# Reciprocal roots in the scan stage of a hybrid encoder block: Ln, Exp and a Newton step in place of GpSimd's power

## The chip, the cores and the metric

The kernel runs on one core of a Trainium2 chip. The core has five instruction queues that run side by side: TensorE (PE in the profile, with its weight loads as PEld), VectorE (DVE), ScalarE (ACT), GpSimd (POOL) and SyncE (SP), which here only issues DMAs. Each queue works in order; a semaphore makes an instruction of one queue wait for one of another. The metric is the device time of one execution in microseconds, as the median of several executions.

## The reference

One layer of a hybrid encoder block on x of 1 x 1024 x 1024 in float32:

```python
h = rmsnorm(x, norm_mix_w)
z, xbc, dt_raw, q, k, v = split(h @ w_in)
y_ssm = ssd_mixer(z, xbc, dt_raw, ...)          # bidirectional scan in chunks of 128
y_na = neighbourhood_attention(q, k, v, ...)    # 16 heads of 64
x = x + concat([y_ssm, y_na]) @ w_out
h = rmsnorm(x, norm_mlp_w)
out = x + square(relu(h @ w_mlp_in)) @ w_mlp_out
```

Two norms inside it matter here. The scan's output is gated and normed by groups of 512 channels, and q and k are normed by heads of 64:

```python
g = y.reshape(bsz, t, SSM_GROUPS, gw) * silu(z).reshape(bsz, t, SSM_GROUPS, gw)
g = g * rsqrt(mean(g * g, axis=-1, keepdims=True) + EPS)     # gw = 512, EPS = 1e-5

q = rmsnorm(q.reshape(bsz, t, NA_HEADS, 64), q_norm_w) * 64 ** -0.5
k = rmsnorm(k.reshape(bsz, t, NA_HEADS, 64), k_norm_w)
```

## The kernel before

The 1024 tokens are eight blocks of 128, one token to a partition. Float32 products are made of three matmuls on operands split into a high and a low part (`mm3`, L177 to L180): ScalarE copies the high part, VectorE or GpSimd subtracts it to get the low one (L148 and L149 for weights, L184 to L190 for what comes out of PSUM).

The work goes in stages. First the norm of x and its transposes; then the projection of the convolved channels and the decays (`decays`, where Exp, Ln and Exp run on ScalarE at L386, L410 and L416); then the projection of z, sixteen blocks whose output goes through Silu (L509). After that comes the stage that the change touches. Two kinds of work run in it together:

- The scan. Eight steps of `backward` and `forward` (L677 to L680), each for two groups. A `backward` step loads the running sums of the decays (`rb`, L605), subtracts on GpSimd (L612), selects on VectorE (L618), takes Exp on ScalarE (L623), multiplies on VectorE (L625) and multiplies by the inputs on TensorE (`pd`, L630). `carried` brings in the state of the chunk before (`py`, then `yo`, L567), `decay_state` makes the next one (`xw` on GpSimd at L653 or L672, `pS` on TensorE, `st` at L549 and L550, its split at L553 and L554). Where both directions have come together, `gated` multiplies by the gate (L574), squares and sums on ScalarE (L576), takes the reciprocal root (`ry`, one number to a token), scales (L578) and stores. It runs sixteen times, in the second half of the scan.
- The projections of q, k and v (`qkv_proj`), 48 blocks of 24 matmuls each into PSUM tiles `pq`, of which three are in rotation. Each of the 32 blocks of q and k goes through `normed_split`: Square on ScalarE (L695), a reduction over each head on VectorE (L697), the reciprocal root (`rq`, eight numbers to a token), the scaling on VectorE that reads `pq` for the last time (L699), four transposes on TensorE (`ptq`, L705) and a split (L187, L188). ScalarE's queue then issues the stores (L717, L723, L732).

Both reciprocal roots come from `inv_rms` (L199 to L203): two GpSimd instructions, a scale-and-add (L201) and a power with exponent -0.5 (L202). The same function serves the norm ahead of the MLP (`r0`, L1080), which the change leaves as it is.

The order of each engine's instructions is not written out in the kernel. A scheduler that comes with the language works it out when the kernel is built, from the order of the program's lines as priority and from its own estimate of each instruction's time (`schedule_with_timeline_sim=True`, L1373); `tc.issue_after(ins)` puts what is traced under it behind `ins` on that engine. So on TensorE the scan's matmuls and the projections' stand interleaved in one fixed order, and a matmul whose operand comes late holds up all behind it. The neighbourhood attention, the output projection and the MLP follow after about 670 us.

ScalarE holds one set of function tables at a time; where the next function isn't in it, the build puts in a table load (`ACT_TABLE_LOAD`).

Of the kernel before, what the change touches and what calls it, by code (L numbers as in the profile page):

```python
# [9 lines left out]
F32 = mybir.dt.float32  # L10
# [3 lines left out]
AF = mybir.ActivationFunctionType  # L14
# [4 lines left out]
P = 128  # L19
# [7 lines left out]
EPS = 1e-5  # L27
NEG = -1.0e30
HD = 64


def shape_constants():
# [23 lines left out]
def hymba_block(  # L56
# [25 lines left out]
    nc = tc.nc  # L82
    mul, add, sub = ALU.mult, ALU.add, ALU.subtract
# [22 lines left out]
    def ps_mm(name="mm"):  # L106
        return phase["ps"].tile([P, 512], F32, tag="mm", name=name, bufs=phase["mm"])

    def ps_tp(name="tp"):
        return ps.tile([P, 512], F32, tag="tp", name=name, bufs=2)  # L110
# [6 lines left out]

    q_dr = dr.tile([8, 4, HD, T], F32, name="q_dr")
    k_dr = dr.tile([2, 2, 4, P, T], F32, name="k_dr")
    v_dr = dr.tile([NT, P, 16, 2, HD], F32, name="v_dr")  # L120
    sz_dr = dr.tile([NT, P, D], F32, name="sz_dr")
# [32 lines left out]
    def load_w_nat(src, r0, nk, c0, lo_eng):  # L154
        tiles = []
        for k2 in range(nk // 2):
            v = src[r0 + 256 * k2 : r0 + 256 * (k2 + 1), c0 : c0 + 512]
            tiles.append(load_w(v.rearrange("(a p) f -> p a f", p=P), lo_eng))

        def get(k):  # L160
            hi, lo = tiles[k // 2]
            s = slice((k % 2) * 512, (k % 2) * 512 + 512)
            return hi[:, s], lo[:, s]

        return get
# [11 lines left out]
    def mm3(pt, ah, al, bh, bl, first, last):  # L177
        nc.tensor.matmul(pt, lhsT=ah, rhs=bh, start=first, stop=False)  # L178
        nc.tensor.matmul(pt, lhsT=ah, rhs=bl, start=False, stop=False)  # L179
        return nc.tensor.matmul(pt, lhsT=al, rhs=bh, start=False, stop=last)  # L180

    def split_from_psum(hi, lo, src, scalar=None):
        if scalar is None:
            nc.scalar.activation(hi, src, AF.Copy)  # L184
            nc.vector.tensor_tensor(lo, src, hi.bitcast(F32), op=sub)
        else:
            nc.scalar.activation(hi, src, AF.Copy, scale=scalar)  # L187
            nc.vector.scalar_tensor_tensor(  # L188
                lo, src, scalar, hi.bitcast(F32), op0=mul, op1=sub
            )  # L190
# [8 lines left out]
    def inv_rms(pool, ss, n, width, tag):  # L199
        r = pool.tile([P, width], F32, tag=tag, name=tag, bufs=2)  # L200
        nc.gpsimd.tensor_scalar(r, ss, 1.0 / n, EPS, op0=mul, op1=add)  # L201
        nc.gpsimd.tensor_tensor(r, r, half[:, 0:width], op=ALU.pow)  # L202
        return r  # L203

    def transpose_split(th, tl, t, hn):
# [13 lines left out]
    with ExitStack() as ph:  # L219
        enter_phase(ph, 1, 3, 1)  # L220
        hp = ph.enter_context(tc.tile_pool(name="hp", bufs=1))
# [15 lines left out]
        rcol = cp.tile([P, NT], F32, name="rcol")  # L237
# [48 lines left out]
        for j in range(2):  # L286
            nc.sync.dma_start(prow[80:81, j * HD : (j + 1) * HD], q_norm_w)
            nc.sync.dma_start(prow[81:82, j * HD : (j + 1) * HD], k_norm_w)
        pp = ps_tp("pp")
# [3 lines left out]
        nc.vector.tensor_scalar(  # L293
            pcol[:, 80:81], pcol[:, 80:81], HD**-0.5, None, op0=mul
        )
# [15 lines left out]
        with ExitStack() as p1:  # L311
            qp = p1.enter_context(tc.tile_pool(name="qp", bufs=2, side="right", reuse_waits="tile"))

            rrow = qp.tile([P, T], F32, name="rrow", bufs=1)
            for h in range(2):
# [5 lines left out]
                    op=mul,  # L321
# [179 lines left out]
            for g in range(2):  # L501
                get = load_w_nat(w_in[0], 0, KD, OFF_Z + 512 * g, nc.vector)
                for t in range(NT):
                    pt = ps_mm("pz")
                    for k in range(KD):
                        s = (slice(None), k, slice(t * P, (t + 1) * P))
                        mm3(pt, hTh[s], hTl[s], *get(k), k == 0, k == KD - 1)
                    zs = qp.tile([P, 512], F32, tag="zs", name="zs")
                    nc.scalar.activation(zs, pt, AF.Silu, scale=rcol[:, t : t + 1])  # L509
                    nc.scalar.dma_start(szb[:, t, :, g * 512 : (g + 1) * 512], zs)  # L510

        def hb(v):
            return v.unsqueeze(2).broadcast_to([P, 8, HD])

        def h8(v):
            return v.rearrange("p (e d) -> p e d", d=HD)

        with ExitStack() as p2:
            qp = p2.enter_context(tc.tile_pool(name="qs", bufs=2, side="right", reuse_waits="tile"))
            zt = qp.tile([P, 192], F32, tag="y1", name="zt")  # L520
            nc.gpsimd.memset(zt, 0.0)
            for r0 in (0, 23):
# [47 lines left out]
            def gated(y1, c, g):  # L570
                gs = slice(g * 512, (g + 1) * 512)
                sz = qp.tile([P, 512], F32, tag="sz", name="sz")
                nc.sync.dma_start(sz, sz_dr[c, :, gs])
                nc.vector.tensor_tensor(y1, y1, sz, op=mul)  # L574
                ss = qp.tile([P, 1], F32, tag="ss", name="ss")
                nc.scalar.activation(sz, y1, AF.Square, accum_out=ss)  # L576
                r = inv_rms(qp, ss, 512, 1, "ry")
                nc.scalar.activation(y1, y1, AF.Copy, scale=r)  # L578
                nc.scalar.dma_start(y_dr[c, :, gs], y1)

            def backward(c, g):
# [61 lines left out]
                if c >= NT // 2:  # L643
                    nc.scalar.dma_start(y1_dr[c, :, g * 512 : (g + 1) * 512], y1)
                else:
                    if c > 0:
                        yf = qp.tile([P, 512], F32, tag="yo", name="yf", bufs=1)
                        nc.sync.dma_start(yf, y1_dr[c, :, g * 512 : (g + 1) * 512])
                        nc.gpsimd.tensor_tensor(y1, y1, yf, op=add)
                    gated(y1, c, g)  # L650
# [42 lines left out]
            def normed_split(pt, rt, w):  # L693
                qn = hp.tile([P, 512], F32, tag="qn", name="qn", bufs=2)
                nc.scalar.activation(qn, pt, AF.Square, scale=rt)  # L695
                ss = hp.tile([P, 8], F32, tag="sq", name="sq", bufs=2)
                nc.vector.tensor_reduce(ss, h8(qn), axis=mybir.AxisListType.X, op=add)  # L697
                r = inv_rms(hp, ss, HD, 8, "rq")
                nc.vector.scalar_tensor_tensor(  # L699
                    h8(qn), h8(pt), rt, hb(r), op0=mul, op1=mul  # L700
                )
                tp = ps_tp("ptq")
                for j in range(4):
                    s = slice(j * P, (j + 1) * P)
                    nc.tensor.transpose(tp[:, s], qn[:, s], ident)  # L705
                hl = hp.tile([P, 2, 512], F32R, tag="hl", name="hl", bufs=2)
                split_from_psum(hl[:, 0], hl[:, 1], tp, w)
                return hl.bitcast(F32).rearrange("f a (p t) -> f a p t", p=4)
# [64 lines left out]
    with ExitStack() as ph:  # L773
# [292 lines left out]
        for t in (0, 4, 1, 5, 2, 6, 3, 7):  # L1066
            xt = x2[:, t, :]
            for h, get in enumerate((get0, get1)):
                pt = ps_mm("po")
                s = slice(t * P, (t + 1) * P)  # L1070
                for k in range(4):
                    yh, yl = last[k]
                    mm3(pt, yh[:, s], yl[:, s], *get(k), k == 0, k == 3)
                d = xt[:, h * 512 : (h + 1) * 512]
                nc.vector.tensor_tensor(d, d, pt, op=add)
            nc.sync.dma_start(x2_dr[t], xt)
            jk = np_.tile([P, D], BF16, tag="jk", name="jk", bufs=1)
            ss = np_.tile([P, 1], F32, tag="ss", name="ss")
            nc.scalar.activation(jk, xt, AF.Square, accum_out=ss)
            r = inv_rms(np_, ss, D, 1, "r0")  # L1080
            nc.vector.scalar_tensor_tensor(xt, xt, r, wb, op0=mul, op1=mul)
            if before is not None:
                factors(before)
            before = t
# [163 lines left out]
    with ExitStack() as ph:  # L1248
# [32 lines left out]
        for fb in range(4):  # L1281
# [18 lines left out]
            for i in ORD:  # L1300
# [14 lines left out]
                for t in range(4):  # L1315
                    pt = (X if i in (1, 6, 7, 4) else Y)[t]
# [60 lines left out]
```

## Time and profile before

| what | us |
|---|---|
| median of three executions | 1728.23 (1726.64 to 1728.27) |
| the profiled execution | 1725.33 |
| its span, from the first instruction to the last | 1723.5 |
| the stage of the change in it | about 270 to 650 |

The span is what the profile's rows are taken from; the 1.8 us between it and the profiled execution's time lie around it. "Busy" is the time in which an engine works on an instruction; "idle before" a group is the time its engine sat unoccupied just ahead of it, and the arrow names what ended most of it. A busy TensorE is not one at its peak, since its matmuls are pipelined and their ends are modelled. Of the chain of work that ended last, which the page follows back from the last instruction, 16% of the span is TensorE's in the MLP.

### The profile page before, as it was taken

To read this page: it belongs to the slowest core of one execution; us is meant where nothing else is said; L and a number is where in the kernel's file an instruction comes from. 1 tells how busy PE (TensorE), PEld (TensorE's weight loads), DVE (VectorE), ACT (ScalarE), POOL (GpSimd) and SP (SyncE) were. 2 spreads that over 40 slices of the span, in tenths; PEclk is the share of its full clock that TensorE was granted. 3 is DMA by queue.
4 is the path that set the end of the run, shared out by engine and by line. 5 is a ranking of instruction groups with operands and counts; after the bars stand their busy time and mean duration, and the time that the engine had idled before them with its cause. 6 is when DMAs were issued, how large, how long until landed. Compare 5 with 4: busy or idle time off the path is not lost. (4 is left out here: it accounts for less than half of the span.)

```text
span 1723.5 us, 20879 instructions
## 1 busy us (share of the span) xinstructions
PE 1636.0 (95%) x7461; PEld 1304.6 (76%) x7461; DVE 1106.3 (64%) x1687; ACT 726.5 (42%) x1189; POOL 705.6 (41%) x496
## 2 busy tenths in 40 slices
PE   6999999989888999999999988999999978999999
PEld 5788888777766777777767767788888866888887
DVE  5767214889787744778787776454343359787863
ACT  5434223434344434555565533454444443333330
POOL 4000004888778741221242242244444426555551
PEclk9999999999998999999999999999999989999999
DMA  8213338876675796754453141254344394644231
GB/s 200 62 37 104 89 98 242 210 195 207 213 206 161 234 311 199 240 150 138 132 183 123 56 159 49 73 190 153 134 159 147 125 349 149 201 141 166 92 110 73
DMA packets 178499, 269.75 MB, mean 157 GB/s; under 512 B 13963, under 2 KB 105051, under 8 KB 178395
## 3 DMA queue, kind: packets, MB, share of 16 engines
q1 hardware_dynamic: 135419, 231.18, 42.6%
q10 hardware_dynamic: 42976, 37.23, 7.1%
q8 instruction: 59, 0.97, 0.2%
q14 instruction: 45, 0.37, 0.1%
HBM read 185.21 MB, written 86.50 MB: 158 GB/s over the span
## 5 line engine op out<-in xcount | busy, mean ns | idle before, releaser
L760 POOL TENSOR_TENSOR wl<-wraw,wh 128x1024 fp32r<-128x1024 f32 x110 | 300.1, 2740 | 350.1 <-ACT wh L759 336.7
L745 PE MATMUL px<-wh,ahl 128*128 128x512 f32 x512 | 163.7, 397 | 9.8 <-ACT ahl L759 9.8
L759 ACT ACTIVATE wh<-wraw 128x1024 fp32r<-128x1024 f32 x110 | 115.7, 1054 | 127.4 <-issue 42.4
L179 PE MATMUL pq<-wl,hTh 128*128 128x512 f32 x384 | 153.1, 400 | 4.6 <-DVE wl L149 4.4
L745 PE MATMUL px<-h,wh 128*128 128x512 f32 x496 | 156.5, 396 | 0.0
L178 PE MATMUL pq<-wh,hTh 128*128 128x512 f32 x384 | 153.1, 401 | 1.9 <-ACT wh L148 1.2
L180 PE MATMUL pq<-wh,hTl 128*128 128x512 f32 x384 | 151.9, 396 | 0.0
L759 ACT ACTIVATE ahl<-ar 128x1024 fp32r<-128x1024 f32 x56 | 58.9, 1053 | 173.0 <-PE px L745 89.6
L760 DVE TENSOR_TENSOR ahl<-ar,ahl 128x1024 fp32r<-128x1024 f32 x56 | 107.3, 1917 | 37.4 <-ACT ahl L759 36.2
L745 PEld LDWEIGHTS px<-wh,ahl 128*128 128x128 f32 x512 | 97.3, 190 | 31.9 <-ACT ahl L759 10.2
L745 PEld LDWEIGHTS px<-h,wh 128*128 128x128 f32 x496 | 93.4, 189 | 22.4
L149 DVE TENSOR_TENSOR wl<-wraw,wh 128x1024 fp32r<-128x1024 f32 x40 | 55.0, 1376 | 83.3 <-ACT wh L148 82.7
L878 POOL TENSOR_TENSOR mb<-braw,nam 128x256 f32<-128x256 f32 (+1 forms) x48 | 41.0, 884 | 159.7 <-DVE nmx L936 123.4
L184 ACT ACTIVATE pth<-ptp 128x384 fp32r<-128x384 f32 (+1 forms) x128 | 58.4, 459 | 107.8 <-PE ptp L959 106.8
L745 PE MATMUL px<-wl,ahl 128*128 128x512 f32 x256 | 100.9, 394 | 0.0
L745 PE MATMUL px<-h,wl 128*128 128x512 f32 x248 | 98.1, 396 | 0.0
L179 PEld LDWEIGHTS pq<-wl,hTh 128*128 128x128 f32 x384 | 73.2, 191 | 22.1 <-DVE wl L149 7.9
L149 POOL TENSOR_TENSOR wl<-wraw,wh 128x1024 fp32r<-128x1024 f32 x18 | 43.8, 2446 | 110.5 <-ACT wh L148 84.3
L745 PE MATMUL pz<-wh,ahl 128*128 128x512 f32 x256 | 82.8, 400 | 6.5 <-DVE acc L1330 5.0
L178 PEld LDWEIGHTS pq<-wh,hTh 128*128 128x128 f32 x384 | 72.9, 190 | 18.2 <-ACT wh L148 2.5
L180 PEld LDWEIGHTS pq<-wh,hTl 128*128 128x128 f32 x384 | 73.2, 191 | 14.7
L612 POOL TENSOR_TENSOR rb<-rb,c 128x512 f32<-128x512 f32 x64 | 75.0, 1192 | 21.5 <-DMA rb<-cum_dr 18.7
(265 smaller groups left out, 4242.6 us busy)
## 6 DMA issues: line engine op xcount, KB each, us to landing
act_dr<-cq SPq DMA_DIRECT2D x56, 512.0 KB, 3.0
ar<-act_dr SPq DMA_DIRECT2D x56, 512.0 KB, 3.8
wraw<-in_w_in_dram SPq DMA_DIRECT2D x44, 512.0 KB, 4.0
rb<-cum_dr SPq DMA_DIRECT2D x32, 512.0 KB, 7.6
wraw<-in_w_mlp_in_dram SPq DMA_DIRECT2D x32, 512.0 KB, 4.7
wraw<-in_w_mlp_out_dram SPq DMA_DIRECT2D x32, 512.0 KB, 5.3
q_dr<-hl ACTq DMA_DIRECT2D x64, 128.0 KB, 3.2
k_dr<-hl ACTq DMA_DIRECT2D x16, 512.0 KB, 3.2
```

The source lines that it names most:

```text
L149: lo_eng.tensor_tensor(lo[:, 0:n], raw[:, 0:n], hi[:, 0:n].bitcast(F32), op=sub)
L178: nc.tensor.matmul(pt, lhsT=ah, rhs=bh, start=first, stop=False)
L179: nc.tensor.matmul(pt, lhsT=ah, rhs=bl, start=False, stop=False)
L180: return nc.tensor.matmul(pt, lhsT=al, rhs=bh, start=False, stop=last)
L184: nc.scalar.activation(hi, src, AF.Copy)
L612: nc.gpsimd.tensor_tensor(rb[:, d], rb[:, d], c1[:, d, c, h0 : h0 + 4].unsqueeze(2).broadcast_to([P, 4, P]), op=sub,)
L745: nc.tensor.matmul(pt, lhsT=a, rhs=b, start=f, stop=l, skip_group_check=True)
L759: nc.scalar.activation(hl[0], src, AF.Copy)
L760: eng.tensor_tensor(hl[1], src, hl[0].bitcast(F32), op=sub)
L878: nc.gpsimd.tensor_tensor(mb[:, s].rearrange("p (s r c) -> p s r c", r=16, c=8), v[:, a:b], nam[:, s].rearrange("p (s r c) -> p s r c", r= ...
```

## The change

A second function for the reciprocal root is added, and the two norms of the scan stage call it. It takes ln of the mean square plus EPS, then exp of -0.5 times that, and improves the result r of the argument s by one Newton step, r (1.5 - 0.5 s r r). `ss` is written over on the way. Ahead of it all, a load of the table set with number 6 (`LN_EXP`), which serves both functions, is put on ScalarE behind the last Silu of the z projection.

```diff
+LN_EXP = 6
...
+    def inv_rms_newton(pool, ss, n, width, tag):
+        r = pool.tile([P, width], F32, tag=tag, name=tag, bufs=2)
+        nc.vector.tensor_scalar(ss, ss, 1.0 / n, EPS, op0=mul, op1=add)
+        nc.scalar.activation(r, ss, AF.Ln)
+        nc.scalar.activation(r, r, AF.Exp, scale=-0.5)
+        nc.vector.scalar_tensor_tensor(ss, ss, -0.5, r, op0=mul, op1=mul)
+        nc.vector.tensor_tensor(ss, ss, r, op=mul)
+        nc.vector.scalar_tensor_tensor(r, ss, 1.5, r, op0=add, op1=mul)
+        return r
...
-                    nc.scalar.activation(zs, pt, AF.Silu, scale=rcol[:, t : t + 1])
+                    last_silu = nc.scalar.activation(zs, pt, AF.Silu, scale=rcol[:, t : t + 1])
...
+            with tc.issue_after(last_silu.ins):
+                nc.scalar.add_instruction(
+                    mybir.InstLoadActFuncSet(
+                        act_func_set_id=LN_EXP,
+                        name=nc.get_next_instruction_name(),
+                        engine=mybir.EngineType.Activation,
+                    )
+                )
...
-                r = inv_rms(qp, ss, 512, 1, "ry")
+                r = inv_rms_newton(qp, ss, 512, 1, "ry")
...
-                r = inv_rms(hp, ss, HD, 8, "rq")
+                r = inv_rms_newton(hp, ss, HD, 8, "rq")
```

## The prediction

> **What bounds the kernel now.** The page comes first: its busy shares, then the span in 40 slices of 43 us, from which these rows matter.
>
> ```profile
> PE 1636.0 (95%) x7461; PEld 1304.6 (76%) x7461; DVE 1106.3 (64%) x1687; ACT 726.5 (42%) x1189; POOL 705.6 (41%) x496
> ...
> PE   6999999989888999999999988999999978999999
> ...
> DVE  5767214889787744778787776454343359787863
> ...
> POOL 4000004888778741221242242244444426555551
> ```
>
> TensorE is busy nearly everywhere. Slices 7 to 14 (about 270 to 650 us) are the scan stage: there PE drops to 8 while VectorE and GpSimd both stand at 7 and 8. So PE sets the pace and this stage makes it wait. The next view is the busy time of each engine in stretches (columns: stretch and length, then busy us and instructions of PE, PEld, DVE, ACT, POOL; granted clock; DMA).
>
> ```profile
> 270.00:430.00 160.00, 147.66 (x730) 119.16 (x730) 129.21 (x193) 61.48 (x104) 127.05 (x112) 1.00 0.79 224
> 430.00:490.00 60.00, 53.18 (x248) 41.39 (x247) 48.65 (x68) 25.25 (x46) 40.53 (x39) 1.00 0.68 207
> 490.00:610.00 120.00, 106.77 (x499) 85.71 (x498) 89.96 (x135) 48.69 (x93) 99.65 (x98) 0.94 0.70 207
> 610.00:650.00 40.00, 39.34 (x181) 31.31 (x180) 17.58 (x21) 14.66 (x22) 13.65 (x15) 1.00 0.94 298
> ```
>
> PE is idle for 12.3 + 6.8 + 13.2 + 0.7 = 33.1 us of these 380. That is all that a change of the norms can give back in the stage. Summed in the same way, DVE is busy 285.4 us and idle 94.6, POOL is busy 280.9, ACT 150.1. Who ends PE's idle time is in the list of waits, cut to 270 to 650 us (us in total, times, longest).
>
> ```profile
> PE pcb L587 <- DVE yo L567: 7.5, 4, 3.1
> PE pd L630 <- DVE rb L625: 7.3, 9, 1.3
> PE pq L179 <- DVE wl L149: 4.4, 5, 1.7
> PE py L178 <- DVE yo L567: 2.5, 2, 2.0
> PE ptq L705 <- DVE qn L699: 1.8, 5, 0.9
> ```
>
> The largest waits all end with a VectorE instruction, and only the last row, 1.8 us, is the norm's own consumer. So the question is what makes VectorE late. There are two kinds of lateness; the timeline has an example of each.
>
> ```profile
> 360.51 1.68 POOL L202 TENSOR_TENSOR rq<-rq,half 128x8 f32<-128x8 f32 x1
> ...
> 362.23 0.75 DVE L699 SCALAR_TENSOR_TENSOR qn<-pq,rcol,rq 128x512 f32<-128x512 f32 x1 [0.93 <-POOL rq L202]
> ...
> 363.03 0.66 PE L705 MATMUL ptq<-ident,qn 128*128 128x128 f32 x4 [0.94 <-DVE qn L699]
> ```
>
> Here a power on GpSimd ends, VectorE had sat 0.93 us for it, and TensorE 0.94. This kind the change removes.
>
> ```profile
> 407.47 0.67 DVE L697 TENSOR_REDUCE sq<-qn 128x8 f32<-128x512 f32 x1
> ...
> 408.06 1.46 DVE L149 TENSOR_TENSOR wl<-wraw,wh 128x1024 fp32r<-128x1024 f32 x1
> ...
> 409.58 0.50 PE L179 MATMUL pq<-wl,hTh 128*128 128x512 f32 x1 [1.73 <-DVE wl L149]
> ```
>
> Here VectorE had no idle time: it worked its queue off, and TensorE lost 1.73 us to a weight's split that came behind a norm's reduction. This kind the change feeds.
>
> **The change, part by part.** Removed from GpSimd, from the groups by line (count, then busy us, mean ns, idle before):
>
> ```profile
> L202 POOL TENSOR_TENSOR rq<-rq,half 128x8 f32<-128x8 f32 x32 | 54.4, 1701 | 1.7
> L201 POOL TENSOR_SCALAR rq<-sq 128x8 f32<-128x8 f32 x32 | 13.2, 413 | 17.5 <-DVE sq L697 15.4
> L202 POOL TENSOR_TENSOR ry<-ry,half 128x1 f32<-128x1 f32 x16 | 10.2, 637 | 0.8
> L201 POOL TENSOR_SCALAR ry<-ss 128x1 f32<-128x1 f32 x16 | 6.9, 434 | 2.8 <-ACT sz L576 1.5
> ```
>
> That is 84.7 us, 30% of POOL's 280.9, in 48 chains. What VectorE gets back is read from the waits that POOL ends on it in the same stretch:
>
> ```profile
> DVE rb L618 <- POOL rb L612: 16.6, 15, 2.5
> DVE qn L699 <- POOL rq L202: 13.8, 17, 2.1
> DVE y L642 <- POOL y L641: 12.3, 6, 4.5
> DVE y L574 <- POOL y L649: 7.0, 4, 3.5
> DVE y L574 <- POOL y L666: 2.6, 2, 1.4
> ```
>
> The 13.8 us are the power itself. The other 38.5 are GpSimd's scan work; I give the powers their share of that queue, 30% or 11.6 us. Together 25.4 of VectorE's 94.6 idle us, 27%. If TensorE's idle time follows VectorE's in proportion, 27% of 33.1 is **8.9 us gained**. The floor is the direct row, 1.8 us. I take 8.9, because the floor leaves out all that waited behind a power in GpSimd's queue.
>
> Added: per chain, four VectorE and two ScalarE instructions. The nearest rows:
>
> ```profile
> L597 DVE SCALAR_TENSOR_TENSOR cf<-dt,cd,dsk x16: 208/228/1002, 273.9 to 589.1; 128x8 f32<-128x8 f32 x16
> ...
> L597 DVE SCALAR_TENSOR_TENSOR cf<-dt,cd,dsk 128x8 f32<-128x8 f32 x16 | 7.1, 444 | 0.3
> L388 DVE TENSOR_SCALAR nega<-nega 128x32 f32<-128x32 f32 x1 | 0.2, 170 | 0.0
> L398 DVE SCALAR_TENSOR_TENSOR pl<-pl,t 128x256 f32<-128x256 f32 x7 | 2.9, 418 | 0.1
> L387 ACT ACTIVATE nega<-nega 128x32 f32<-128x32 f32 x1 | 0.2, 229 | 0.0
> ```
>
> L597 is the same operation on the same shape in the same stage (min/median/max ns, then busy us and mean): 208 ns at least, 444 in the mean, so some of the 16 take three or four times the least. Three two-operand instructions cost 3 x 208 to 3 x 444 ns, the scale-and-add 170: 0.79 to 1.50 us a chain, 38 to 72 us over 48 chains. I take 300 ns each, nearer the median than the mean because GpSimd, whose work these long ones run beside, loses 30% of its load: 1.07 us a chain, 51 us in all. The L398 row, seven dependent instructions with 0.1 us idle before them, says that the dependence adds almost nothing. TensorE now loses 33.1 / 285.4 = 0.116 us per us of VectorE work; at that rate 51 us are **6.0 us lost** (4.4 to 8.4).
>
> The Trainium skill speaks against this part: "VectorE: DVE Perf Modes", section "Rules for kernel authors", asks to keep the number of chained VectorE instructions low, since each pays its own pipeline flush. The L597 row agrees that eight elements are not cheap; the rule taken alone is rival C below.
>
> The Ln and Exp are two ScalarE instructions of about 0.23 us, 48 x 0.46 = 22 us, on an engine idle 230 of 380 us there: nothing. That cover is thinner than it looks, since ScalarE's queue is in order and often stands on VectorE:
>
> ```profile
> ACT rb L623 <- DVE rb L618: 49.1, 25, 5.7
> ...
> ACT y L578 <- POOL ry L202: 18.5, 9, 4.0
> ```
>
> A Ln queued behind L623 waits up to 5.7 us, and VectorE's last three instructions, with everything queued behind them (the L149 splits, L625 for pd, L567 for yo), wait with it. Against this stands the old chain's latency, 0.20 + 1.65 us at best and more behind GpSimd's queue; the new one is 1.07 + 0.46 plus two crossings of engines, as before. I cost the swap at nothing, between a gain of the 13.8 us row's share (counted above) and the loss in rival C. The 18.5 us of ScalarE waiting for ry go, but no PE row above ends with it. The explicit table load stands where a load stands already (L623, first Exp of the scan, 280.7 us): nothing.
>
> Sum: -8.9 + 6.0 = -2.9 us. The profiled execution took 1725.33 us (span 1723.5 and 1.8 around it), so 1722.4; it lies 2.9 us under the median of 1728.23, so **1725.3 us** against that median. A measurement of this kernel can tell about 0.2%, 3.5 us, from no change.
>
> **The rivals.**
>
> A, the forecast: gain and loss nearly cancel. With the gain from 1.8 to 8.9 and the loss from 4.4 to 8.4, and a few us for a new order of the queues, its own range is 1718 to 1733. Chance 0.45.
>
> B, GpSimd's queue was the pacer. The instruction order is planned anew, and with 30% less in that queue xw, y and rb come early enough that half of PE's 33.1 us go: 1728.2 - 16.5 = 1712. For it: 52.3 us of VectorE's idle time end on GpSimd, and from 610 to 650 us, where GpSimd is busy 34%, PE loses 0.7 us in 40. Against it: the scan's VectorE work has gone there too. Chance 0.22.
>
> C, VectorE becomes the bound: slower. Its idle time is 94.6 us over 48 chains, 1.97 us a chain, and the new instructions take 0.79 to 1.50 of it. From about 2 us a chain, work plus stalls on Exp, it has nothing left; earlier wherever it already runs without a gap, as at 407 us. If one chain in two falls in such a stretch at 1.07 us, TensorE loses 48 x 1.07 / 2 = 26 us, less 8.9 gained: +17, 1745; with one in three +8, 1736. I take 1741. For it: every large PE wait ends on VectorE. Chance 0.25.
>
> D, the norms are hidden anyway: their only direct PE row is 1.8 us; 1728. Chance 0.04.
>
> E, the change doesn't do what it says, because the table is switched between each Ln and Exp. The trace of before has this pattern in the decays:
>
> ```profile
> 119.95 1.28 ACT L416 ACT_TABLE_LOAD   x1
> 121.24 0.42 ACT L416 ACTIVATE c<-c 128x256 f32<-128x256 f32 x1
> 121.68 1.28 ACT L410 ACT_TABLE_LOAD   x1
> ```
>
> Ln (L416) and the Exp after it (L410) each got a load. Two per chain are 96 x 1.28 = 123 us of ScalarE, under its 230 idle, but 2.6 us more in every chain; a third of it showing is +41: 1769. The Trainium skill, "ScalarE: Activation LUTs", section "Table sets: the hidden batching unit", says that one set holds both functions; the explicit load selects a set once, after the last Silu, and that speaks against E. The same page's "What ACT_TABLE_LOAD costs" puts a switch at 2.66 us with its drain, which would make E 255 us of ScalarE; the trace has no gap beyond 0.02 us ahead of the second load, so it does not show that drain. Chance 0.04.
>
> **How the numbers follow.** Faster by over 0.2%: 0.18 of A and all of B, 0.40. Within 0.2%: 0.17 of A and D, 0.21. Slower: 0.10 of A, C and E, 0.39. The range is to leave out no more than 0.2: it reaches from just under B's 1712 to just over C's 1741, 1709 to 1743, and leaves out E, the far end of C and the far end of B.
>
> **What would show it.** Right: in 270 to 650 us POOL's busy time falls by about 85 us, DVE's rises by about 50, and PE's idle time is near 30 us, still ended by VectorE. The new two-operand instructions have a mean of about 300 ns; at 444 or above the loss was too small. One table load stands between the last Silu and the end. B shows as PE idle near 16 us; C as stretches of VectorE at 9.5 of 10 and above with new waits of VectorE on Exp, each over a microsecond. The granted clock of 0.94 from 490 to 610 us can move a few us either way, and the new order of the queues can shift waits in stages that the change doesn't touch; both would make the prediction wrong without saying anything on the norms.

## The result, and the profile after

The changed kernel takes 1737.57 us (median of seven executions, 1732.49 to 1741.85) against 1727.76 us for the kernel before (seven, 1720.39 to 1728.50). Compared side by side the ratio is **1.0067 (95% interval 1.0052 to 1.0082)**: slower by about 11.6 us (the two medians differ by 9.8). The forecast was 1725.3, so its sign was wrong; rival C with 1741 came nearest. The profiled execution of after took 1732.49 us, the quickest of its seven, against 1725.33 for that of before.

The page of after, in rows that the prediction showed of before:

```profile
PE 1633.7 (94%) x7461; PEld 1302.9 (75%) x7461; DVE 1147.7 (66%) x1879; ACT 741.7 (43%) x1285; POOL 623.8 (36%) x400
...
DVE  5767215989899863778788777453343349886863
...
POOL 4000003556665402211232342144444426555551
```

GpSimd lost 81.8 us, about the 84.7 foreseen, and is at 4 to 6 in the eighth to the fourteenth slice, where it was at 7 and 8. VectorE gained 41.4 us of busy time and is at 8 and 9 in each of these slices. To see where the time is, both traces are cut at the first and the last matmul of the projections (`pq`). The views of busy time in two stretches, the stage and what lies behind it, first of before, then of after (columns as in the prediction: busy us and instructions of PE, PEld, DVE, ACT, POOL; granted clock; DMA share and GB/s):

```profile
268.90:670.60 401.70, 368.65 (x1749) 295.49 (x1748) 289.51 (x419) 155.21 (x270) 283.76 (x264) 0.98 0.74 219
...
670.60:1723.50 1052.90, 1014.78 (x4557) 801.76 (x4555) 682.08 (x1118) 468.51 (x787) 400.39 (x192) 0.98 0.44 148
```

```profile
267.30:682.00 414.70, 373.28 (x1749) 299.67 (x1748) 331.52 (x611) 170.61 (x366) 205.22 (x168) 0.97 0.71 212
...
682.00:1730.40 1048.40, 1008.78 (x4556) 796.98 (x4554) 682.68 (x1118) 468.51 (x787) 398.11 (x192) 0.99 0.45 149
```

The stage became **13.0 us longer**, 414.7 against 401.7. With the same 1749 matmul records TensorE is idle for 414.70 - 373.28 = 41.4 us in it instead of 401.70 - 368.65 = 33.1 (+8.4), and its busy time is 4.6 us more. Behind the stage the same work took 4.5 us less at a granted clock of 0.99 against 0.98. That part is not put down to the change, which does not touch it: over the seven executions of after the mean granted clock goes from about 0.975 to 0.983 and the time from 1742 to 1732, and the profiled one had the highest clock.

Who ends TensorE's idle time in after, 270 to 660 us (us in total, times, longest):

```profile
PE ptq L724 <- DVE qn L718: 9.5, 7, 3.3
PE pq L180 <- DVE wl L150: 5.6, 4, 2.6
PE py L179 <- DVE st L569: 5.6, 4, 3.0
PE pd L649 <- DVE rb L644: 4.9, 7, 1.4
PE ptq L724 <- DVE ry L213: 3.7, 1, 3.7
PE ptq L724 <- DVE sq L211: 3.1, 1, 3.1
PE pcb L606 <- DVE yo L586: 2.8, 3, 1.5
```

Before, the transposes of the normed blocks (`ptq`) had one wait beside the 1.8 us that the prediction shows:

```profile
PE ptq L705 <- ACT sz L576: 0.8, 1, 0.8
```

So the waits at the transposes went from 2.6 us to 9.5 + 3.7 + 3.1 = 16.3. Of the scan's own waits two fell, `pd` from 7.3 to 4.9 and `pcb` from 7.5 to 2.8, and one rose, that of `py` on `st`, from 1.3 to 5.6. TensorE's new idle time lies where the norm hands its block back. This place alone does not name the cause, for e3 below waits 9.5 us at the transposes too and is the quickest kernel of all. VectorE's waits on GpSimd became short:

```profile
DVE rb L637 <- POOL rb L631: 11.6, 8, 2.3
...
DVE y L661 <- POOL y L660: 3.8, 4, 1.4
DVE sq L211 <- ACT rq L210: 2.3, 5, 0.5
DVE y L593 <- POOL y L668: 2.3, 2, 1.2
...
DVE y L593 <- POOL y L685: 0.6, 1, 0.6
```

What GpSimd ends is 18.3 us. Before, it was 53.5: the 52.3 of the prediction's rows and one that they leave out:

```profile
DVE yo L567 <- POOL y L641: 1.2, 1, 1.2
```

The new wait, Newton's first step on Exp, is 2.3 us in all, at most 0.5 at a time. VectorE hardly stands still for the norm's Exp; it has a queue. What it now does, in groups by line (count, busy us, mean ns, idle before):

```profile
L211 DVE SCALAR_TENSOR_TENSOR sq<-sq,rq 128x8 f32<-128x8 f32 x32 | 12.2, 381 | 2.4 <-ACT rq L210 2.3
L213 DVE SCALAR_TENSOR_TENSOR rq<-sq,rq 128x8 f32<-128x8 f32 x32 | 12.0, 375 | 0.5
...
L208 DVE TENSOR_SCALAR sq<-sq 128x8 f32<-128x8 f32 x32 | 10.2, 317 | 0.3
L212 DVE TENSOR_TENSOR sq<-sq,rq 128x8 f32<-128x8 f32 x32 | 9.9, 309 | 0.3
L211 DVE SCALAR_TENSOR_TENSOR ss<-ss,ry 128x1 f32<-128x1 f32 x16 | 5.0, 312 | 0.1
L212 DVE TENSOR_TENSOR ss<-ss,ry 128x1 f32<-128x1 f32 x16 | 4.6, 290 | 0.2
L213 DVE SCALAR_TENSOR_TENSOR ry<-ss,ry 128x1 f32<-128x1 f32 x16 | 4.4, 273 | 0.3
L208 DVE TENSOR_SCALAR ss<-ss 128x1 f32<-128x1 f32 x16 | 2.3, 147 | 0.9 <-ACT sz L595 0.9
```

The durations sum to 60.6 us, 1.26 us a chain. Neighbours overlap, so the stage's busy time rose by less, 331.5 - 289.5 = 42.0. The sum is not all work. 37 of the 192 instructions took over 0.4 us, 34.8 us together, and by the records of both engines each of these 37 began while a GpSimd instruction was running and ended 15 to 32 ns behind the end of that one. About half of the added time is VectorE held until GpSimd is done. One place in the timeline of after shows how they hurt (start, duration, instruction, idle before):

```profile
554.20 1.50 POOL L691 TENSOR_TENSOR xw<-xs,wd 128x512 f32<-128x512 f32 x1
...
554.78 0.94 DVE L211 SCALAR_TENSOR_TENSOR sq<-sq,rq 128x8 f32<-128x8 f32 x1
...
555.64 0.67 DVE L716 TENSOR_REDUCE sq<-qn 128x8 f32<-128x512 f32 x1
...
556.24 0.68 DVE L593 TENSOR_TENSOR y<-y,sz 128x512 f32<-128x512 f32 x1
556.84 0.15 DVE L212 TENSOR_TENSOR sq<-sq,rq 128x8 f32<-128x8 f32 x1
...
557.05 0.15 DVE L213 SCALAR_TENSOR_TENSOR rq<-sq,rq 128x8 f32<-128x8 f32 x1
...
557.25 0.75 DVE L718 SCALAR_TENSOR_TENSOR qn<-pq,rcol,rq 128x512 f32<-128x512 f32 x1
...
558.14 0.63 PE L724 MATMUL ptq<-ident,qn 128*128 128x128 f32 x4 [3.71 <-DVE ry L213]
```

TensorE had nothing since 554.43 and waits for `qn` (L718; the releaser named, `ry` L213, is a neighbour that ended at about the same time). VectorE is busy throughout. It has two q or k chains and one of the scan in its queue at once. Newton's first step for this block (L211) takes 0.94 us, until GpSimd's L691 has ended at 555.70 us, and the second step (L212) stands behind another block's reduction and a gate of 0.68 us. Between reduction and scaling the old chain had no instruction in VectorE's queue; the new one has four.

What such a stall costs does not end with it. Three stretches of after, from 554.4 us:

```profile
554.40:558.10 3.70, 0.03 (x1) 0.00 (x0) 3.70 (x13) 1.96 (x8) 1.29 (x1) 1.00 0.32 97
558.10:562.00 3.90, 3.86 (x13) 3.17 (x14) 3.90 (x15) 3.00 (x8) 0.56 (x1) 0.61 0.41 144
562.00:566.00 4.00, 4.00 (x26) 3.55 (x26) 4.00 (x8) 2.17 (x4) 3.77 (x3) 0.96 0.70 134
```

Behind 3.7 idle us come 3.9 us in which the granted clock is 0.61 and TensorE gets through 13 matmuls; in the next four it does 26. The clock's records show windows of 3.41 us, or a multiple, at exactly half rate: four in the stage of before, the equal of eight in that of after, each of these beginning in a stall of 1.36 to 3.71 us or up to 1.6 us behind it (one of the four of before has no stall of even 1 us near it). Stalls of TensorE of 1.3 us or more in the stage went from 5 to 11. The Trainium skill, "TensorE: Matmul & The Clock Gate", section "Part 1: The HAM clock gate", has this window as 3413 ns, and the records agree; it also asks for an idle window of about 3.4 us before the clock falls, and this trace has it fall at shorter ones, as here, at a stall of 1.36 us on `wl` that ends at 337.5 us:

```profile
337.40:340.80 3.40, 3.30 (x11) 2.72 (x11) 3.40 (x7) 1.75 (x6) 0.80 (x1) 0.55 0.76 179
```

### The profile page after: what moved, and what is told of

Same layout as the page of the kernel before. It is cut to its first block, busy times and chain, and to the rows that moved or that the text cites. A ratio compares the mean times of both kernels' runs of the same rounds, so it can differ in the third digit from the quotient of the medians.

```text
span 1730.4 us, 21076 instructions
## 1 busy us (share of the span) xinstructions
PE 1633.7 (94%) x7461; PEld 1302.9 (75%) x7461; DVE 1147.7 (66%) x1879; ACT 741.7 (43%) x1285; POOL 623.8 (36%) x400
## 5 line engine op out<-in xcount | busy, mean ns | idle before, releaser
L779 DVE TENSOR_TENSOR ahl<-ar,ahl 128x1024 fp32r<-128x1024 f32 x56 | 110.1, 1968 | 36.0 <-ACT ahl L778 34.8
```

The source lines that it names most:

```text
L779: eng.tensor_tensor(hl[1], src, hl[0].bitcast(F32), op=sub)
```

## The experiments

Two theories stood at first. **Load**: the new instructions fill VectorE, wherever they stand. **Length** ("chain theory" in the expectations): the way from reduction to scaling got longer, so the block comes back too late. As rivals: the table load, the ScalarE instructions, and mere change of order ("order theory"), since the scheduler plans the instructions anew for every edit. "Busy" and "idle" below are of the stage, cut as above; "way" is the mean time from the reduction's end to the scaling's start over the 32 blocks of q and k, worked out from both instructions' records: 5.10 us before, 6.50 after. Ratios are to the kernel before, with 95% intervals. Columns of the rows are those of the stretches above.

### The change in parts

e1_ry_only: `ry` alone by the new chain (against after).

```diff
-                r = inv_rms_newton(hp, ss, HD, 8, "rq")
+                r = inv_rms(hp, ss, HD, 8, "rq")
```

> Only the scan's norm (ry, 16 chains) takes Ln, Exp and Newton; q's and k's (rq, 32 chains) go back to GpSimd's power. Load theory (the loss is VectorE's new instructions, 60.6 us in the changed kernel, at which TensorE then waits): ry's share is 16.3 us of the 60.6, so about a quarter of the 11.6 us lost stays, +3 us on before (ratio 1.002). Chain theory (the loss is the longer way from the reduction to the scaling in normed_split, for which the transposes wait): none of it stays, 1.000. TensorE's wait for qn at the transposes is near 2 us by the chain theory, some 4 by the load theory.

e2_rq_only: `rq` alone.

```diff
-                r = inv_rms_newton(qp, ss, 512, 1, "ry")
+                r = inv_rms(qp, ss, 512, 1, "ry")
```

> Only q's and k's norms take Ln, Exp and Newton; the scan's norm keeps GpSimd's power. Load theory: 44.3 of 60.6 us of VectorE's new work stay, +8.5 us on before (1.005). Chain theory: the whole loss stays, +11.6 us (1.007), and TensorE's waits at the transposes stay near 16 us. The two are near each other here; with e1 the sum tells whether the loss adds up or sits in rq alone.

Measured: e1 1.0032 (1.0018 to 1.0046), e2 1.0125 (1.0105 to 1.0144). The stage of e2:

```profile
267.70:689.20 421.50, 380.77 (x1741) 305.68 (x1740) 318.52 (x545) 164.91 (x332) 223.51 (x200) 0.95 0.69 209
```

Both parts cost, and nearly all of it comes with the 32 chains of q and k (way in e2 6.64 us, in e1 5.05). They don't add: 0.32% + 1.25% is more than the 0.67% of both together. TensorE's idle time in e2, 40.7 us, is that of after; what e2 has on top is clock, 0.95 against 0.97 over the stage. Why it lost more clock with the same idle time isn't settled. Both theories expected less of e2 (1.005 and 1.007), and neither lets a part of the change lose 0.58% more than the whole.

e6_table_only: the kernel before with the table load alone, both calls back to `inv_rms`.

```diff
-                r = inv_rms_newton(qp, ss, 512, 1, "ry")
+                r = inv_rms(qp, ss, 512, 1, "ry")
...
-                r = inv_rms_newton(hp, ss, HD, 8, "rq")
+                r = inv_rms(hp, ss, HD, 8, "rq")
```

> The kernel before with the load of the table set that serves Ln and Exp behind the last Silu, and nothing else of the change: it takes the place of the load ahead of the scan's first Exp. Load and chain theory: 1.000. Order theory: whatever a new order costs; if this one is off 1.000 by 0.3% or more, single orders differ by that much and no small difference of the other runs can be read.

Measured: 0.9994 (0.9979 to 1.0009). The table load costs nothing that can be told from zero. The stage:

```profile
267.40:671.30 403.90, 372.85 (x1749) 298.75 (x1748) 292.58 (x419) 155.32 (x270) 282.80 (x264) 0.97 0.73 218
```

This kernel takes the same time as before, and yet its one trace has TensorE idle for 31.1 us instead of 33.1 and busy for 372.9 instead of 368.7, with the equal of seven windows at half rate instead of four. Differences of this size between two traces can't be put down to an edit.

### The chain on other engines

e3_act_only: the scale and EPS inside Ln, no Newton step; nothing of the chain on VectorE or GpSimd. It leaves out the Newton step.

```diff
+    nc.gpsimd.memset(half[:, 7:8], EPS)
+    epsc = half[:, 7:8]
...
-        nc.vector.tensor_scalar(ss, ss, 1.0 / n, EPS, op0=mul, op1=add)
-        nc.scalar.activation(r, ss, AF.Ln)
+        nc.scalar.activation(r, ss, AF.Ln, scale=1.0 / n, bias=epsc)
         nc.scalar.activation(r, r, AF.Exp, scale=-0.5)
-        nc.vector.scalar_tensor_tensor(ss, ss, -0.5, r, op0=mul, op1=mul)
-        nc.vector.tensor_tensor(ss, ss, r, op=mul)
-        nc.vector.scalar_tensor_tensor(r, ss, 1.5, r, op0=add, op1=mul)
```

> The Newton step is left out, and scale and EPS go into Ln's own scale and bias: two ScalarE instructions and nothing on VectorE or GpSimd. Load theory: VectorE's load is that of before, GpSimd's is 85 us less, so the gain that was forecast shows, 3 to 9 us below before (0.995 to 0.998). Chain theory: the way from reduction to scaling falls from 5.1 us to about 2, the transposes wait 1 us or less, 5 us or more below before (0.997 or less). Order theory (any new order of the queues costs some us, whatever the instructions): no better than before, 1.000 to 1.007.

Measured: **0.9975 (0.9960 to 0.9991)**, 1720.7 us, the quickest kernel of this study. Its stage:

```profile
268.90:668.00 399.10, 370.57 (x1753) 299.28 (x1752) 291.29 (x420) 175.83 (x367) 203.35 (x168) 0.97 0.73 220
```

Idle time is 28.5 us, 4.6 less than before, and the way 3.87 us. With GpSimd relieved of the power and nothing put on VectorE for it, the kernel is 4.3 us (0.25%) quicker. Whether that is the relief or the new order is not shown: e10 below, with still less to do, gains nothing.

e4_no_newton: the scale-and-add stays on VectorE, Newton is left out.

```diff
-        nc.vector.scalar_tensor_tensor(ss, ss, -0.5, r, op0=mul, op1=mul)
-        nc.vector.tensor_tensor(ss, ss, r, op=mul)
-        nc.vector.scalar_tensor_tensor(r, ss, 1.5, r, op0=add, op1=mul)
```

> Only the Newton step's three VectorE instructions are left out; the scale-and-add on VectorE, Ln and Exp stay. Load theory: 12.5 us of the 60.6 stay, so within 2 us of before plus a part of the gain, 0.997 to 1.001. Chain theory: the way from reduction to scaling is about 3.5 us against 5.1, so 2 to 5 us below before (0.997 to 0.999). Order theory: 1.000 to 1.007, as the changed kernel.

Measured: 1.0022 (1.0004 to 1.0041), between e3 and after as the number of VectorE instructions in the chain is (none, one, four). But the first instruction would cost 0.47% and the next three 0.45% together, so these steps are not the price of single instructions.

e8_newton_pool: the scale-and-add and Newton on GpSimd, five instructions; Ln and Exp on ScalarE.

```diff
-        nc.vector.tensor_scalar(ss, ss, 1.0 / n, EPS, op0=mul, op1=add)
+        nc.gpsimd.tensor_scalar(ss, ss, 1.0 / n, EPS, op0=mul, op1=add)
...
-        nc.vector.scalar_tensor_tensor(ss, ss, -0.5, r, op0=mul, op1=mul)
-        nc.vector.tensor_tensor(ss, ss, r, op=mul)
-        nc.vector.scalar_tensor_tensor(r, ss, 1.5, r, op0=add, op1=mul)
+        nc.gpsimd.tensor_tensor(ss, ss, r, op=mul)
+        nc.gpsimd.tensor_tensor(ss, ss, r, op=mul)
+        nc.gpsimd.tensor_scalar(ss, ss, -0.5, 1.5, op0=mul, op1=add)
+        nc.gpsimd.tensor_tensor(r, ss, r, op=mul)
```

> The changed kernel with its scale-and-add and Newton step on GpSimd (five instructions there, since it has no scalar_tensor_tensor here, of some 0.2 us) and Ln and Exp on ScalarE: nothing new on VectorE, but the way from reduction to scaling stays long, at 5 to 8 us. Load theory: 0.9975 to 1.000. Chain theory: 1.004 to 1.010 with TensorE waiting 10 us and more at the transposes.

Measured: 1.0071 (1.0051 to 1.0090), the same as after. The stage:

```profile
265.80:685.90 420.10, 378.33 (x1749) 305.52 (x1748) 288.85 (x419) 169.57 (x366) 269.28 (x408) 0.95 0.70 209
```

VectorE has not one instruction more than before (419), GpSimd is busy for less than before (269.3 us against 283.8), and the stage is 5.4 us longer than in after. VectorE's load can't be the whole cause: the way is 7.32 us here, which speaks for a price of length.

### Load without length, and length without load

e5_dve_load: the kernel before with four VectorE instructions more a chain, whose results nobody reads.

```diff
+        nc.vector.tensor_scalar(u, ss, 1.0 / n, EPS, op0=mul, op1=add)
+        nc.vector.scalar_tensor_tensor(u, ss, -0.5, u, op0=mul, op1=mul)
+        nc.vector.tensor_tensor(u, ss, u, op=mul)
+        nc.vector.scalar_tensor_tensor(u, ss, 1.5, u, op0=add, op1=mul)
```

> The kernel before with its GpSimd power, and beside each of the 48 chains four more VectorE instructions of the same forms as the change's, whose result nobody reads. Load theory: from the kernel without any of them on VectorE (0.9975) to the changed one (1.0067) 60.6 us of them cost 15.9 us, 0.26 us per us; here the same on top of before, 1.009. Chain theory: the way from reduction to scaling grows only by the queueing, 1.000 to 1.003. Order theory: 1.000 to 1.007.

e7_act_and_load: the same four on top of e3.

> The version with Ln and Exp alone (scale and EPS in the Ln, no Newton step), and beside each chain the four VectorE instructions off the chain. Load theory: the load of the changed kernel without its longer chain, 1.0067 as the changed kernel. Chain theory: 0.9975 to 1.000, as without them, and the way from reduction to scaling near 4 us.

Measured: e5 1.0082 (1.0063 to 1.0101), e7 1.0128 (1.0106 to 1.0150). The stage of e5:

```profile
266.80:685.40 418.60, 377.64 (x1757) 306.52 (x1756) 318.81 (x613) 157.01 (x272) 280.82 (x264) 0.95 0.70 210
```

Four instructions a chain, with the power still on GpSimd, cost as much as the whole change. But they are written into the tile of the scaling's result, so the scaling comes behind them, and the way grew with them (e5 6.81 us, e7 6.12): these two hold load and length at once, and e7 lost more than either theory expected.

e9_act_load_in_scan: on top of e3, twelve unread instructions in each `backward` step, away from the norms; 192 in all, as many as the change adds.

```diff
+                u = half[:, 4:7]
+                for _ in range(3):
+                    nc.vector.tensor_scalar(u, cf[:, 0:3], 1.0 / 512, EPS, op0=mul, op1=add)
+                    nc.vector.scalar_tensor_tensor(u, cf[:, 0:3], -0.5, u, op0=mul, op1=mul)
+                    nc.vector.tensor_tensor(u, cf[:, 0:3], u, op=mul)
+                    nc.vector.scalar_tensor_tensor(u, cf[:, 0:3], 1.5, u, op0=add, op1=mul)
```

> The version with Ln and Exp alone, and in each of the sixteen backward steps of the scan twelve small VectorE instructions (192, as many as the change adds, of the same forms on 3 columns), whose result nobody reads: VectorE's load of the changed kernel, and none of it between a reduction and its scaling, where the four per chain of the earlier load runs stood. Load theory (any VectorE time costs): 1.005 to 1.013. Chain theory (only what stands between reduction and scaling costs): 0.997 to 1.001 and the way from reduction to scaling near 4 us.

e13_double_load: the same with `range(6)`, 384 instructions.

> As the version with Ln and Exp alone and twelve idle VectorE instructions in each backward step, now with twenty-four: 384 instructions, about 111 us, none between a reduction and its scaling. Load theory: the cost grows with the dose, and steeper as VectorE fills (338 of 411 us with twelve): 1.012 to 1.025. Order theory (the 1.0044 was one planned order against another): no growth with the dose, 0.998 to 1.006.

Measured: e9 1.0044 (1.0027 to 1.0061), e13 1.0145 (1.0125 to 1.0166); way 4.08 us in both. The stage of e9, then of e13:

```profile
267.70:678.70 411.00, 372.60 (x1749) 298.56 (x1748) 337.78 (x611) 174.77 (x366) 204.45 (x168) 0.97 0.71 214
```

```profile
266.90:696.80 429.90, 382.47 (x1749) 306.77 (x1748) 368.84 (x803) 172.66 (x366) 195.06 (x168) 0.94 0.69 205
```

This is load by itself, for the norms' way stayed as in e3, within 0.2 us. The first 192 instructions raise VectorE's busy time from 291.3 to 337.8 us and cost 0.69% or 11.9 us over e3: 11.9 / 46.5 = **0.26 us per us**. The next 192 add 31.1 us of busy time and 17.4 us: 0.56 per us. Over both doses it is 29.3 us for 77.6, or 0.38. That the price rises with the dose is likely and not shown, for 17.4 and 11.9 us differ by no more than the order of the queues can move (e10).

e11_long_act_chain: on top of e3, six copies of the factor by ScalarE behind Exp; nothing on VectorE.

```diff
+        for _ in range(6):
+            nc.scalar.activation(r, r, AF.Copy)
```

> The version with Ln and Exp alone, and six copies of the factor onto itself on ScalarE behind the Exp in each chain (about 0.2 us each, 58 us in all on the engine that is idle over half of the stage): a longer chain with nothing on VectorE or GpSimd. Load theory of VectorE: 0.9975 to 0.999. Chain theory: the way from reduction to scaling grows from 3.9 to above 5.5 us, 1.004 to 1.008, like the changed kernel and the one with its Newton step on GpSimd.

e14_double_act_chain: the same with `range(12)`.

> As the version with six copies of the factor on ScalarE behind the Exp, now with twelve: the way from reduction to scaling grows from 6.8 to 8.5 us or more, ScalarE's load by another 55 us. Chain theory: 1.007 to 1.015. Order theory: no growth with the length, 0.998 to 1.004.

Measured: e11 1.0026 (1.0014 to 1.0038), e14 1.0138 (1.0120 to 1.0155). The stage of e11, then of e14:

```profile
265.90:669.60 403.70, 371.51 (x1741) 300.54 (x1740) 288.95 (x417) 213.43 (x652) 202.61 (x168) 0.96 0.73 218
```

```profile
267.70:697.40 429.70, 376.73 (x1749) 304.23 (x1748) 283.95 (x419) 246.19 (x942) 193.63 (x168) 0.94 0.68 205
```

With nothing more on VectorE the kernel loses as the way grows: from 3.87 to 6.84 us of way 0.51%, 8.8 us; from there to 10.98 another 1.12%, 19 us. In e14 TensorE waits for the scaling as the theory says: 23.9 us at the transposes, against 9.5 in e3. In e11 it waits 3.8 us there, less than in e3, so that e11's loss is not shown to be length. ScalarE's own queue is fuller too (175.8 us busy in e3, 213.4 in e11, 246.2 in e14), so some of both losses can be that.

### Bounds on the gain

e10_no_chain: the factor is a constant 1, and nothing of the chain runs.

```diff
-                r = inv_rms(qp, ss, 512, 1, "ry")
+                r = one[:, 0:1]
...
-                r = inv_rms(hp, ss, HD, 8, "rq")
+                r = one
```

> The kernel before with the chains left out: the norm's factor is a constant 1, so no instruction on any engine between the reduction and the scaling, and q, k and the scan's output are not normed. It bounds what the norms' instructions cost in any form. Both theories: below the version with Ln and Exp alone, 0.990 to 0.997; if it is at 0.9975 like that one, nothing is left to gain here, and TensorE's idle time has other causes.

Measured: 1.0009 (0.9996 to 1.0023).

```profile
266.70:666.50 399.80, 372.75 (x1741) 302.45 (x1740) 291.15 (x417) 155.60 (x268) 199.66 (x168) 0.96 0.72 220
```

Both theories expected a gain here, and there is none. With no reciprocal roots at all the idle time falls to 27.1 us (the way is 0.63 us), yet the kernel is not quicker than before. It does less than e3 and takes 0.34% longer. What is left to differ is the order of the queues, and the clock that goes with where the stalls fall. So these are worth some 0.3% by themselves, by e2 perhaps more, and differences of that size between two kernels aren't to be put down to single instructions.

e12_act_wl_pool: on top of e3, the low parts of the weights of q, k and v (L152 there) go to GpSimd.

```diff
-                get = load_w_nat(w_in[0], 0, KD, off + 512 * g, nc.vector)
+                get = load_w_nat(w_in[0], 0, KD, off + 512 * g, nc.gpsimd)
```

> The version with Ln and Exp alone, and the low parts of the weights of q, k and v (24 tiles, 1.4 us each on VectorE) subtracted on GpSimd instead (2.4 us each), which lost 85 us of work: VectorE has 33 us less in the stage. Load theory: 33 us at 0.26 us per us are 8 us less, 0.993. Chain theory: 0.996 to 0.998, a few us by less queueing. A loss would mean that TensorE then waits for the weights' low parts on GpSimd.

Measured: 1.0081 (1.0065 to 1.0098), slower. The stage:

```profile
266.50:685.60 419.10, 382.30 (x1757) 309.01 (x1756) 285.78 (x396) 176.19 (x369) 254.89 (x192) 0.94 0.69 210
```

Both theories expected a gain. TensorE does not wait long for the low parts on GpSimd (2.2 us). VectorE lost 24 instructions of some 1.5 us, but only 5.5 us of busy time. Where much of the rest went stands in its groups in the stage, first of e3, then of e12:

```profile
L571 DVE TENSOR_TENSOR sl<-st,sh 128x512 fp32r<-128x512 f32 x28 | 26.0, 929 | 1.3 <-ACT sh L570 1.2
L191 DVE SCALAR_TENSOR_TENSOR hl<-ptq,pcol,hl 128x512 fp32r<-128x512 f32 x32 | 23.6, 741 | 4.6 <-ACT hl L190 4.6
...
L558 DVE TENSOR_TENSOR xl<-xw,xh 128x512 fp32r<-128x512 f32 x28 | 23.1, 825 | 9.0 <-ACT xh L557 9.0
```

```profile
L571 DVE TENSOR_TENSOR sl<-st,sh 128x512 fp32r<-128x512 f32 x28 | 33.3, 1191 | 0.3 <-ACT sh L570 0.3
L558 DVE TENSOR_TENSOR xl<-xw,xh 128x512 fp32r<-128x512 f32 x28 | 32.0, 1143 | 10.3 <-ACT xh L557 10.3
L191 DVE SCALAR_TENSOR_TENSOR hl<-ptq,pcol,hl 128x512 fp32r<-128x512 f32 x32 | 23.8, 743 | 25.0 <-ACT hl L190 25.0
```

The same subtractions of two tiles in SBUF take 1191 and 1143 ns instead of 929 and 825; the one that reads PSUM (L191) stays at 0.74 us. The records show how. Of the 28 at L571, 15 take about 0.68 us; the other 13 began while a GpSimd instruction was running and ended 0.55 us behind its end, however long that took (in e3 it is 8 of 28, in the same way). Those held by one of the moved subtractions (L152) take 2.2 to 2.9 us. It is not GpSimd's busy time as such: before has more of it (283.8 us against 254.9), and its mean for the first of these groups (L554 there) is 856 ns. So part of what goes to GpSimd in large pieces comes back as VectorE held, and this kernel doesn't test what less load on VectorE is worth. TensorE's busy time is 11.7 us over e3's (clock 0.94), its idle time 8.3 us.

## Why the prediction was wrong

**What bounds the kernel: right.** TensorE sets the pace, and the change acts through its idle time in this stage, which VectorE's instructions end, before and after.

**The gain, 8.9 us: too large.** GpSimd's busy time fell by about 80 us, as the working said, and VectorE's waits on it from 53.5 to 18.3 us, more than the 25.4 given back. But TensorE's idle time didn't follow in proportion: in e3, where only the relief is left, it fell by 4.6 us, and the kernel gained 4.3; in e10, which has no chain at all, the kernel gained nothing. So the term was between nothing and about 4. That VectorE's waits on GpSimd were mostly slack, which its queue made up again, is the likely reading and not shown. The trace of before does show that the powers were not what held VectorE's other work: the 28 instructions of L541, L554, L563 and L574 that began while a power ran took 0.27 to 0.69 us, as they do alone, while nearly all that began during a 128x512 instruction of GpSimd waited for its end.

**The loss, 6.0 us: the step that failed.** The work itself was sized well: 51 us forecast, 60.6 by the sum of durations, 42.0 of busy time. The mean of the two-operand instructions, (12.2 + 12.0 + 9.9 + 5.0 + 4.6 + 4.4) us / 144 = 334 ns, is near the 300 taken, though few are that long: half take under 0.17 us, and those that GpSimd held make the mean. What was wrong was the rate. 0.116 us per us was the average of before: all idle time of TensorE over all work of VectorE. An addition pays the marginal rate, and that was 0.26 far from the norms (e9) and 0.38 over the double dose (e13). At 0.26 the 51 us are 13 us lost instead of 6.0, and the sum has the other sign. That additions cost is clear of the order: each of the eleven kernels that add VectorE instructions or a longer way (after, e1, e2, e4, e5, e7, e8, e9, e11, e13, e14) has its whole interval above 1, and the three that add nothing (e3, e6, e10) lie at 0.9975 to 1.0009; e12, which moves work to GpSimd, is a case of its own. How much each adds is known to some 0.3%, no better.

**The swap of the waits, at nothing: likely failed too.** Priced was the wait on Exp, and that was right: 2.3 us. What was missed is that four instructions in sequence each take a place in VectorE's queue between reduction and scaling, while the old chain took none there. The way grew by 1.4 us where it could have shrunk (3.87 in e3). That length costs rests on e8, without a VectorE instruction more, and on e14, where the transposes wait 23.9 us; near the change's own length there is only e11, 8.8 us for 3.0, which the order and ScalarE's fuller queue could have made. By e9 and e11 the step from e3 to after should cost 0.69% for the load and 0.51% x 2.63 / 2.97 = 0.45% for the way, 1.14%; measured is 0.92%. The two shares can't be told apart better than that.

**The clock, left to chance: open.** Of the stage's 13.0 us more, 4.6 are not idle time but slower matmuls, by the traces of before and after. The forecast and rival C priced idle time alone. But e6, which is as quick as before, has nearly the busy time of after (372.9 us against 373.3), and against it after differs by idle time only, 41.4 us against 31.1. So one trace of each kernel doesn't show that the change costs clock.

**The table load and ScalarE's work, at nothing: right.** e6 measures 0.9994; Ln and Exp took 195 to 206 ns each in the groups. After has one load behind the last Silu, so rival E falls.

**The rivals.** B falls: GpSimd was relieved more than enough, and neither after nor e10 came near 1712. D, hidden norms, is half right: the power was nearly hidden, its replacement isn't. C had the place, VectorE's queue, and almost the size, the latter in part by luck: of its signs, VectorE without a gap showed in places (554.4 to 566 us), but waits on Exp of over a microsecond each didn't. Nor does the loss need VectorE without idle time: it comes at 331.5 busy of 414.7 us, 80%. A's own range ended too low: its terms of 1.8 gained and 8.4 lost make 1734.8, not 1733.

**Open:** why e2 and e12 lose more clock than after at less idle time; what share the order that the scheduler found has in any difference under some 0.3%, and in that of e2; and how the 11.6 us divide between load, length and order.

## What to carry to other kernels

An addition to the engine on which the bounding engine's waits end is priced at the marginal rate, measured by a dose of idle work put there, not at the average of waits over work; and work taken from a queue whose waits are mostly hidden gains only what that queue truly held up. Two kernels whose instruction order was planned anew can differ by 0.3% for that alone, so an addition is tried at one dose and at two. On a chain that goes back to the bounding engine, count the places in each in-order queue, not only the durations: here scale and EPS inside Ln, with no step on VectorE, came out at -0.25%, and the change with four small VectorE instructions at +0.67%. Whoever can do without the Newton step tries e3; whoever can't stays with the power on GpSimd.

## What the runs showed of the hardware

Half rate of the clock goes with stalls that are shorter than its windows. Over the stage in all sixteen traces, 30 of 31 stalls of TensorE of 3 us or more touched a window of 3.41 us at half rate (one that began up to 3.5 us after the stall's end or was running then; from the clock's and the matmuls' records), 46 of 56 stalls of 2 to 3 us, 31 of 71 of 1.3 to 2 us and 18 of 64 of 1.0 to 1.3 us. A stretch of the same length at a random place of these stages would do so in 25, 20, 18 and 16 of 100 cases. So the link is plain from 2 us on, weaker from 1.3, and hardly above chance below. A window costs up to half its length, 1.7 us, on top of the stall.

Small VectorE instructions have two kinds of duration. The view of line L211 of after (min/median/max ns, first and last start):

```profile
L211 DVE SCALAR_TENSOR_TENSOR sq<-sq,rq x32: 146/165/1016, 285.6 to 639.0; 128x8 f32<-128x8 f32 x32
...
L211 DVE SCALAR_TENSOR_TENSOR ss<-ss,ry x16: 148/158/1233, 460.0 to 618.6; 128x1 f32<-128x1 f32 x16
```

Half of them take about 0.16 us whether they have eight elements or one, and some take six to eight times that, so that the mean is about twice the median. What makes the long ones is in the records. All 37 of the change's 192 instructions that took over 0.4 us began while GpSimd was at an instruction and ended 15 to 32 ns behind its end. Wider ones are held likewise: a VectorE subtraction of two 128x512 tiles in SBUF takes about 0.68 us, and those that took over 0.7 us began during a GpSimd instruction of 128x512 or 128x1024 and ended 0.55 us behind its end (13 of 28 at L571 in e12, 8 of 28 in e3). GpSimd's powers on 128x8 did not do this in before, and VectorE's split that reads PSUM stayed at 0.74 us. So in these traces what GpSimd runs, and how long each piece is, sets what a small VectorE instruction beside it takes.
